# An attention plan with other costs, a model of transfers, 94 shifted due times, and a new front

## The chip, the cores and the metric

One Trainium2 chip, one of its cores. A core has five engines with a queue of instructions each: PE (matmuls), DVE and ACT and POOL (elementwise work), SP (here only the issue of transfers), and 16 DMA engines that move data between HBM and the on-chip memories. PE writes its results to PSUM, the accumulators; POOL reads only the on-chip SBUF. The metric is the device time of one execution in microseconds (us), as a median over runs.

## The reference

One encoder layer on 512 tokens of width 1024, in float32, with 16 learned meta tokens ahead. Two attention mixers run on the same normalised input, their outputs are gated and merged, and a gated feed-forward network follows:

```python
u = rms_norm(h, pre_mix_gain[l])
proj = u @ w_in[l]
qa, ka, va, qb, kb, vb, g = jnp.split(proj, SPLITS, axis=-1)
# rope on qa (16 heads x 64), ka (4 heads), qb and kb (8 heads x 2 x 64)
o_swa = windowed_gqa_sink_attention(qa, ka, va, attn_sink[l], pos, is_real)
o_diff = differential_attention(qb, kb, vb, lam, lambda_init, diff_subln_gain[l], is_key)
gates = jax.nn.sigmoid(g + b_gate[l])
merged = g_swa * (o_swa @ w_branch_swa[l]) + g_diff * (o_diff @ w_branch_diff[l])
h = h + rms_norm(merged @ w_out[l], post_mix_gain[l])
u = rms_norm(h, pre_ffn_gain[l])
gate_up = u @ w_ffn_in[l]
f = (jax.nn.silu(gate_up[..., :D_FF]) * gate_up[..., D_FF:]) @ w_ffn_out[l]
h = h + rms_norm(f, post_ffn_gain[l])
```

The windowed attention has 4 key/value heads for 16 query heads, a band of three 128-blocks, the meta keys and a sink. The differential attention has 8 heads; each takes two softmaxes, subtracts `lam` times the second from the first, multiplies by V and normalises per head.

## The kernel before, in words

**Numbers.** Each float32 operand is split into a high and a low part: a cast on ACT makes the high part (`wh`, `xh`), a subtraction on DVE or POOL the rest (`wl`, `xl`). A product of two split operands is three matmuls (`mm3`, L287 to L289): high by high, high by low, low by high. A projection is eight such steps into one PSUM tile `pr`, of which there are three.

**The front** (up to L505) is written out in order. 60 small matmuls on zeros (L380) run while the first transfers land. x is loaded in eight pieces and split; the K projection of the windowed mixer follows on PE piece by piece, then two V projections (`wV` into two `tr` tiles, `wV2` by `v2`). In parallel the rows of x (`xn`, `xm`) are loaded and squared for the row norm `rst`, which PE transposes into `rps` and ACT copies to `rbc`; V, Q and K need it.

**The plan.** From L505 to the end of the attention nothing is ordered by hand. The code states tasks (`T(engine, cost, function, reads, writes, ...)`) and `Plan.run` plays them through in time: at each step it takes the engine that can start first, and on it the task with the earliest due time among those that can start within 0.12 us. A task's due time is when it can start plus a slack by its priority (on PE the priority alone). The instructions are then emitted in that order, engine by engine, so the costs set the order and nothing else: on the chip each engine goes through its queue and waits where an operand is missing. Each issue of a transfer also waits until the last transfer of one of eight counters, given out in turn over all queues, has landed.

**What the plan orders.** `v_swa` scales, transposes and splits V; `q_swa` and the K block project, rotate (`rope_t`: two multiplications on DVE, an addition on POOL, a high part on ACT, a low part on DVE) and move the result by SP transfers (`move`) into the layout of the scores. In it Q holds its high part in partitions 0 to 63 and its low part in 64 to 127, and K its high and low part side by side, in both halves. `s_swa` and `t_swa` are scores and output of one of 16 block steps of the windowed mixer, `qk`, `vd`, `s_diff`, `t_diff` the same of a head of the differential one. A step of `s_diff` is four matmuls `Sd`, a minimum on DVE (L868), an exponential on ACT (L871), a reciprocal, for the second softmax a multiplication by `nlam` (L881), and the scaling. `t_diff` transposes four blocks `tr` (L918), splits them into `dah` and `dal`, and multiplies them by V (L931, L933). Gate projections, branch products `b1` and the projections of later heads fill PE between them. `weights` loads a 512 KB weight by an SP issue (L527), casts it on ACT (L529) and subtracts on POOL for each second one, on DVE for the others (L253); `wr` has three buffers, so a load waits until the weight three back has been split.

```python
T("SP", 0.35, lambda: sp.dma_start(out=wr.t, in_=src.rearrange("p (k c) -> p k c", k=KT)),
  w=[wr], dep=dep, prio=pr_, land=3.6 if nfill[0] > 3 else 0.3)
T("ACT", 1.05, lambda: act.copy(out=wh.t, in_=wr.t), r=[wr], w=[wh], prio=pr_)
if nfill[0] % 2:
    T("POOL", 2.65, lambda: sub_hi(wl.t, wr.t, wh.t, pool), r=[wr, wh], w=[wl], prio=pr_, port=True)
```

After the plan come the branch product with `w_bd`, the output projection, the norms and the feed-forward network, which the change leaves alone.

Of the kernel before, what the change touches and what calls it, by code (L numbers as in the profile page):

```python
# [109 lines left out]
class Task:  # L110
    def __init__(self, n, eng, cost, fn, prio, port, land):
        self.n, self.eng, self.cost, self.fn, self.prio, self.port, self.land = n, eng, cost, fn, prio, port, land
        self.deps, self.alloc, self.bufs, self.done, self.start = set(), [], [], None, None


class Plan:
# [6 lines left out]
    AFTER = dict(PE=0.22, ACT=0.07, DVE=0.07, POOL=0.12, SP=0.1)  # L123

    def __init__(self, tags, free):
        self.free = free
        self.slots = {t: [0.0] * n for t, n in tags.items()}
        self.tasks, self.sigs, self.bufs, self.last = [], {}, [], {}
# [19 lines left out]
    def task(self, eng, cost, fn, r=(), w=(), dep=(), keep=(), on=(), sig=None, prio=9, port=False, land=0.0,  # L148
             chain=None):
        k = Task(len(self.tasks), eng, cost, fn, prio, port, land)  # L150
# [25 lines left out]
    def run(self):  # L176
        free = self.free
        port = 0.0
        todo = {e: [k for k in self.tasks if k.eng == e] for e in free}
        self.idle = []  # L180
        while any(todo.values()):
            best = None
            for e, ks in todo.items():
                cand = []
                for k in ks:
                    t = 0.0
                    for d in k.deps:
                        if d.done is None:
                            t = None
                            break  # L190
                        t = max(t, d.done + (0.0 if d.eng == e else self.AFTER[d.eng]))
# [5 lines left out]
                    for tag, n in need.items():  # L197
# [4 lines left out]
                        t = max(t, f[n - 1] + 0.07)  # L202
# [4 lines left out]
                    cand.append((max(t, free[e], port if k.port else 0.0), due, k))  # L207
# [30 lines left out]
def encoder(ctx, tc, I, out, dbg=None):  # L238
# [89 lines left out]
    nlam = const.tile([P, 1], F32, name="nlam")  # L328
    qsc = const.tile([P, 1], F32, name="qsc")
# [49 lines left out]
    for _ in range(60):  # L379
# [41 lines left out]
    nw[0] += 1  # L421
# [19 lines left out]
    for k in range(KT):  # L441
        todo = [(ps_, w[a][:, k, :], (xh, xl)[b][:, k, cs], k == 0 and a == b == 0, k == KT - 1 and a == 1)
                for hs, w in ((kA, wA), (kB, wB)) for ps_, cs in zip(hs, halves) for a, b in ((0, 0), (0, 1), (1, 0))]
        if k == 0:
            todo = [x for p in range(3) for x in todo[p::3]]
        for ps_, a, b, first, last in todo:
            pe.matmul(out=ps_, lhsT=a, rhs=b, start=first, stop=last)
# [42 lines left out]
    v2(1, range(KT))  # L490
# [9 lines left out]
    for c in range(2):  # L500
# [9 lines left out]
                   ta=2, tb=1, vt=1, rt=RT, ma=3), dict(PE=4.3, ACT=0.05, DVE=0.05, POOL=0.0, SP=0.0))  # L510
# [10 lines left out]
    def weights(src, dep=()):  # L521
# [5 lines left out]
        T("SP", 0.35, lambda: sp.dma_start(out=wr.t, in_=src.rearrange("p (k c) -> p k c", k=KT)),  # L527
          w=[wr], dep=dep, prio=pr_, land=3.6 if nfill[0] > 3 else 0.3)
        T("ACT", 1.05, lambda: act.copy(out=wh.t, in_=wr.t), r=[wr], w=[wh], prio=pr_)  # L529
        if nfill[0] % 2:  # L530
            T("POOL", 2.65, lambda: sub_hi(wl.t, wr.t, wh.t, pool), r=[wr, wh], w=[wl], prio=pr_, port=True)
        else:
            T("DVE", 1.23, lambda: sub_hi(wl.t, wr.t, wh.t), r=[wr, wh], w=[wl], prio=pr_, port=True)
        return wh, wl

    def products(w, x, xb, c0, c1, dep=()):
# [3 lines left out]
        for k in range(KT):  # L540
            T("PE", 3 * mm_t(c1 - c0),
              lambda k=k: mm3(pb.t[:, 0:c1 - c0], (wh.t[:, k, :], wl.t[:, k, :]),
                              (x[0][:, k, c0:c1], x[1][:, k, c0:c1]), k == 0, k == KT - 1),
              r=[wh, wl] + xb, w=[pb], dep=dep, prio=20 + nfill[0])
        return pb

    def rope_t(hl, pa, pb, c0, n, p0, o0, scale, more=False):

        ta = sb("ta", [P, 2, HALF], F32, "ta", 2)
        tb = sb("tb", [P, 2, HALF], F32, "tb", 1)  # L550
        m = 2 * n / 528.0

        def half(t, src, i):
            dve.tensor_tensor(out=t.t[:, :, 0:n], in0=src.t[:, p0:p0 + n].unsqueeze(1).broadcast_to([P, 2, n]),  # L554
                              in1=rot[:, i:i + 2, c0:c0 + n], op=ALU.mult)
# [8 lines left out]
        T("DVE", 0.15 + 0.55 * m, lambda: half(ta, pa, 1), r=[pa, ROT], w=[ta], prio=3)  # L564
        T("DVE", 0.15 + 0.55 * m, lambda: half(tb, pb, 0), r=[pb, ROT], w=[tb], prio=3)
# [1044 lines left out]
```

## Time and profile before

| | |
|---|---|
| median of 3 runs | 951.69 us (951.49 to 952.1) |
| the profiled execution | 949.22 us |
| its span, first to last instruction | 947.4 us |
| PE busy | 931.6 us, 98% |
| DVE, ACT, POOL busy | 76%, 55%, 23% |
| HBM | 95 GB/s over the span |

Times in the profile count from the span's start. The profiled execution lies 1.8 us above its span and 2.5 us below the median of the runs. A matmul's time runs from its start to the modelled end of its pipeline, and the next one starts before that end, so the sum of their times is more than PE's busy time. PE is 98% busy: what counts is where PE stands idle or starts late, and not how much the other engines do. The granted clock (PEclk) is full in all 40 slices of the page but one stretch, which the windows show.

### The profile page before, as it was taken

Reading aid. Unit: us, or ns where it says so; the run is one execution under the profiler, and the core shown is the slowest. Engines: PE = TensorE matmul, PEld = TensorE weight load, DVE = VectorE, ACT = ScalarE, POOL = GpSimd, SP = SyncE. Lnnn points to the kernel's source line nnn. Section 1 sums busy time; section 2 is a strip of 40 time slices with the busy share of each in tenths; the row PEclk is TensorE's granted clock in tenths of the full one; section 3 lists DMA queues with packets and bytes.
Section 4 is the critical chain, followed back from the end, with each engine's and each line's share of the span. In section 5 each row is a group of like instructions: output and inputs, shape, how many; then the busy total and the mean of one; then the engine's idle time right before and its main releaser. Section 6 shows DMA issues by size and latency. Waiting matters only on the chain.

```text
span 947.4 us, 15653 instructions
## 1 busy us (share of the span) xinstructions
PE 931.6 (98%) x5871; PEld 834.1 (88%) x5871; DVE 716.2 (76%) x1234; ACT 525.8 (55%) x957; POOL 216.0 (23%) x228
## 2 busy tenths in 40 slices
PE   9999999999999999999999999999999999999996
PEld 9788879889898999999888888998999999988885
DVE  5738898999564759877773865886787887799975
ACT  7337766775644446667556443654555555565541
POOL 0544455543222433243211421300000000000000
PEclk9999999999999999999999999999999999999999
DMA  9483132251425144433532460364323333180122
GB/s 319 160 220 102 51 104 58 63 148 45 123 89 157 46 122 127 105 96 115 157 112 67 161 216 23 100 186 141 117 104 101 117 95 112 46 333 13 55 67 89
DMA packets 38011, 110.46 MB, mean 117 GB/s; under 512 B 6177, under 2 KB 7457, under 8 KB 37937
## 3 DMA queue, kind: packets, MB, share of 16 engines
q1 hardware_dynamic: 37792, 109.34, 38.1%
q8 instruction: 46, 0.75, 0.3%
q14 instruction: 29, 0.23, 0.1%
q10 hardware_dynamic: 144, 0.13, 0.0%
HBM read 88.09 MB, written 2.10 MB: 95 GB/s over the span
## 4 chain that ended last, share of the span: by engine, by line
PE 86%; DVE 5%; DMA 4%; ACT 2%; issue 1%; SPq 1%; DVEq 0%; ACTq 0%
PE pr L287 19%; PE pr L289 19%; PE pr L288 19%; PE Sd L863 3%; PE wk L288 2%; PE wk L287 2%; PE wk L289 2%; PE Sw L715 2%; PE O L771 2%; PE tr L918 2%; PE Od L931 2%; PE tr L764 2%; DMA wr<-in_w_in_dram 2%; PE tr L288 1%; PE tr L287 1%; PE tr L289 1%
## 5 line engine op out<-in xcount | busy, mean ns | idle before, releaser
L287 PE MATMUL pr<-xh,wh 128*128 128x264 f32 (+1 forms) x592 | 193.4, 327 | 0.0
L289 PE MATMUL pr<-xh,wl 128*128 128x264 f32 (+1 forms) x592 | 190.0, 321 | 0.6 <-POOL wl L253 0.6
L288 PE MATMUL pr<-xl,wh 128*128 128x264 f32 (+1 forms) x592 | 189.8, 321 | 0.0
L253 POOL TENSOR_TENSOR wl<-wr,wh 128x1024 fp32r<-128x1024 f32 (+2 forms) x42 | 99.5, 2372 | 145.2 <-ACT wh L529 82.5
L289 PEld LDWEIGHTS pr<-xh,wl 128*128 128x128 f32 x592 | 111.6, 189 | 9.6 <-POOL wl L253 1.3
L288 PEld LDWEIGHTS pr<-xl,wh 128*128 128x128 f32 x592 | 111.9, 189 | 7.4
L287 PEld LDWEIGHTS pr<-xh,wh 128*128 128x128 f32 x592 | 111.8, 189 | 7.4 <-issue 0.2
L529 ACT CAST wh<-wr 128x1024 fp32r<-128x1024 f32 x56 | 58.5, 1048 | 47.0 <-PE pr L288 34.6
L309 POOL TENSOR_TENSOR r3y<-r3v,mhalf 128x1 f32<-128x1 f32 x4 | 2.2, 549 | 326.1 <-DVE r3v L308 326.1
L253 DVE TENSOR_TENSOR wl<-wr,wh 128x1024 fp32r<-128x1024 f32 (+2 forms) x61 | 69.0, 1134 | 10.0 <-ACT wh L272 8.2
L287 PE MATMUL pr<-TM,sx 128*128 128x256 f32 x236 | 66.9, 283 | 0.2 <-ACT s L1393 0.2
L289 PE MATMUL pr<-TM,sx 128*128 128x256 f32 x236 | 66.8, 283 | 0.0
L288 PE MATMUL pr<-TM,sx 128*128 128x256 f32 x236 | 66.8, 283 | 0.0
L868 DVE TENSOR_REDUCE nm<-Sd 128x1 f32<-128x528 f32 x64 | 45.1, 705 | 20.8 <-PE Sd L863 19.9
L253 DVE TENSOR_TENSOR sx<-S,sx 128x1024 fp32r<-128x1024 f32 x34 | 41.6, 1224 | 24.9 <-PE pr L288 12.7
L289 PE MATMUL pr<-uh,wl 128*128 128x256 f32 (+1 forms) x188 | 55.0, 292 | 0.4 <-DVE wl L253 0.4
L287 PE MATMUL pr<-uh,wh 128*128 128x256 f32 (+1 forms) x188 | 55.0, 293 | 0.0
L288 PE MATMUL pr<-ul,wh 128*128 128x256 f32 (+1 forms) x188 | 54.9, 292 | 0.0
L566 POOL TENSOR_TENSOR ta<-ta,tb 128x528 f32<-128x528 f32 (+1 forms) x26 | 37.0, 1422 | 74.5 <-DVE tb L554 45.3
L871 ACT ACTIVATE pp<-Sd,nm 128x528 f32<-128x528 f32 x40 | 27.9, 699 | 39.2 <-DVE pa L884 22.6
L257 ACT CAST sx<-S 128x1024 fp32r<-128x1024 f32 x34 | 35.7, 1050 | 25.1 <-PE pr L289 8.2
L729 POOL TENSOR_SCALAR p<-p,rc 128x272 f32<-128x272 f32 (+1 forms) x64 | 35.9, 573 | 47.9 <-DVE rc L727 44.5
(528 smaller groups left out, 2673.9 us busy)
## 6 DMA issues: line engine op xcount, KB each, us to landing
wr<-in_w_in_dram SPq DMA_DIRECT2D x50, 512.0 KB, 4.1
wg<-in_w_fi_dram SPq DMA_DIRECT2D x17, 512.0 KB, 3.6
wu<-in_w_fi_dram SPq DMA_DIRECT2D x17, 512.0 KB, 3.5
wr<-in_w_fi_dram SPq DMA_DIRECT2D x16, 512.0 KB, 3.8
b<-in_w_fo_dram SPq DMA_DIRECT2D x16, 512.0 KB, 8.5
Kd<-hl SPq DMA_DIRECT2D x32, 132.0 KB, 2.4
Kd<-Kd SPq DMA_DIRECT2D x16, 264.0 KB, 3.7
Q<-hl SPq DMA_DIRECT2D x64, 64.0 KB, 2.8
```

What stands on the lines that cost most here:

```text
L253: (eng or dve).tensor_tensor(out=lo, in0=src, in1=hi.bitcast(F32), op=ALU.subtract)
L257: act.copy(out=hi, in_=src)
L287: pe.matmul(out=ps, lhsT=ah, rhs=bh, start=first, stop=False, **more)
L288: pe.matmul(out=ps, lhsT=ah, rhs=bl, start=False, stop=False, **more)
L289: pe.matmul(out=ps, lhsT=al, rhs=bh, start=False, stop=last, **more)
L529: T("ACT", 1.05, lambda: act.copy(out=wh.t, in_=wr.t), r=[wr], w=[wh], prio=pr_)
L566: T("POOL", 0.05 + 1.3 * m, lambda: pool.tensor_tensor(out=ta.t[:, :, 0:n], in0=ta.t[:, :, 0:n], in1=tb.t[:, :, 0:n], op=ALU.add), r=[tb], ...
L715: pe.matmul(out=Sw2[S.slot][:, 0:nk], lhsT=QS[g][hh].t[:, i * P:(i + 1) * P], rhs=KB[g].t[:, x, r0:r1], start=(x == 0), stop=(x == 1))
L729: T("POOL", 0.2 + 0.43 * c, lambda z=z: pool.tensor_scalar(out=pt.t[:, z, 0:nk], in0=pt.t[:, z, 0:nk], scalar1=rc.t[:, z:z + 1], scalar2=1 ...
L863: pe.matmul(out=S.t[:, s, 0:HALF], lhsT=Q[c].t[:, i * P:(i + 1) * P], rhs=K[c].t[:, x, s * HALF:(s + 1) * HALF], start=(x == 0), stop=(x = ...
L868: T("DVE", 0.71, lambda S=S, c=c, one=one: dve.tensor_reduce(out=nm.t[:, c, one], in_=S.t[:, :, 0:HALF], axis=AX.XY, op=ALU.min), r=[S], w ...
L871: T("ACT", 0.9, lambda S=S, c=c, one=one, p=p: act.activation(out=p().rearrange("p (a b) -> p a b", a=2), in_=S.t[:, :, 0:HALF], func=AF.E ...
```

## The change

**Plan.** The cost of nearly every task is another. The single landing time per transfer is replaced by one queue for transfers (`xfer`): each starts 1.2 us after its issue at the earliest, behind the one before, and lands 0.45 us after its service. The delay from engine to engine (`AFTER`) becomes `lag`, with a drain of 0.165 us for PE. 94 tasks get a shift of their due time (`SHIFT`).

**Weights.** From the fourth on, ACT issues the plan's weight loads and no longer SP (55 of 58). POOL's subtraction is cut into four quarters, and a product's k-th step waits for its quarter alone.

**Attention.** K's low part is no longer copied to partitions 64 to 127, and the second score matmul takes partitions 0 to 63 alone, which leaves out the product of the two low parts. The multiplication by `nlam` on DVE becomes a scaling of the denominator by `ilam` = 1/`nlam` on ACT ahead of the reciprocal. The copy of V's meta rows moves from DVE to ACT. K's rotation comes behind V. The first two `w_bd` products stand in the plan, and the second V half's products too.

**Front.** 41 small matmuls for 60; K's weights from an array that the host has laid out anew, both columns of a k together; V's weight in two halves.

```diff
@@ Plan
-    AFTER = dict(PE=0.22, ACT=0.07, DVE=0.07, POOL=0.12, SP=0.1)
+    OVER = dict(PE=0.0, ACT=0.098, DVE=0.083, POOL=0.03, SP=0.0)
+    DRAIN = dict(PE=0.165, ACT=0.0, DVE=0.0, POOL=0.0, SP=0.0)
+    SHIFT = (
+        "39:2.27 71:16 98:-0.25 104:2.63 115:8 178:78 217:6 226:0.81 242:-8 251:2 262:0.35 290:-0.48 292:3.44 "
...
+    def lag(a, b):
+        return (0.77 if a == "SP" else 0.27) if b == "PE" else 0.06 if b == "SP" else 0.092 if b == "POOL" and a in ("ACT", "DVE") else 0.036
...
+                    due += self.shift.get(k.n, 0.0)
...
-            free[k.eng] = t + k.cost
-            k.done = t + k.cost + k.land
+            free[k.eng] = t + max(0.06, k.cost - self.OVER[k.eng]) if k.eng != "PE" else t + k.cost
+            k.done = t + k.cost + k.land + self.DRAIN[k.eng]
+            if k.xfer:
+                queue = max(t + 1.2, queue) + k.xfer
+                k.done = queue + 0.45
@@ front
-    for _ in range(60):
+    for _ in range(41):
         pe.matmul(out=wps[:, 0:P], lhsT=warm, rhs=warm, start=True, stop=True)
...
+    for what in ("x0", "w0", "x1", "x2", "w1", "x3", "x4", "w2", "x5", "x6", "w3", "x7"):
+        n = int(what[1])
+        if what[0] == "w":
+            k_weights(n)
+        else:
+            x_load(n)
+            x_split(n)
...
+    for ks in (slice(0, KT // 2), slice(KT // 2, KT)):
+        sp.dma_start(out=rV[:, ks], in_=I["w_in"][2].rearrange("p (k c) -> p k c", k=KT)[:, ks])
+        split(wV[0][:, ks], wV[1][:, ks], rV[:, ks])
@@ weights
-        T("SP", 0.35, lambda: sp.dma_start(out=wr.t, in_=src.rearrange("p (k c) -> p k c", k=KT)),
-          w=[wr], dep=dep, prio=pr_, land=3.6 if nfill[0] > 3 else 0.3)
+        e, eng, xfer = ("ACT", act, 2.0) if nfill[0] > 3 else ("SP", sp, 0.0)
+        T(e, 0.38, lambda: eng.dma_start(out=wr.t, in_=src.rearrange("p (k c) -> p k c", k=KT)), w=[wr], dep=dep,
+          prio=pr_, land=0.7, xfer=xfer)
...
-            T("POOL", 2.65, lambda: sub_hi(wl.t, wr.t, wh.t, pool), r=[wr, wh], w=[wl], prio=pr_, port=True)
+            parts = []
+            for q in range(4):
+                ks = slice(2 * q, 2 * q + 2)
+                parts.append(T("POOL", 0.69, lambda ks=ks: sub_hi(wl.t[:, ks], wr.t[:, ks], wh.t[:, ks], pool), r=[wr, wh],
+                               keep=[wl], prio=pr_))
@@ K
-        move(lambda K=K: K.t[64:128], lambda K=K: K.t[0:64], [], [K], land=4.0)
+            move(lambda K=K: K.t[64:128, 0], lambda K=K: K.t[0:64, 0], [], [K], 0.7)
@@ s_diff (s_swa likewise)
-                            pe.matmul(out=S.t[:, s, 0:HALF], lhsT=Q[c].t[:, i * P:(i + 1) * P],
-                                      rhs=K[c].t[:, x, s * HALF:(s + 1) * HALF], start=(x == 0), stop=(x == 1))
+                            pe.matmul(out=S.t[:, s, 0:HALF], lhsT=Q[c].t[0:P - 64 * x, i * P:(i + 1) * P],
+                                      rhs=K[c].t[0:P - 64 * x, x, s * HALF:(s + 1) * HALF], start=(x == 0), stop=(x == 1))
...
+                if c:
+                    T("ACT", 0.2, lambda one=one: act.activation(out=den.t[:, 1, one], in_=den.t[:, 1, one], func=AF.Copy,
+                                                                 scale=ilam), w=pw, on=["lam"], prio=0)
...
-                    T("DVE", 0.16, lambda one=one: dve.tensor_tensor(out=rc.t[:, 1, one], in0=rc.t[:, 1, one], in1=nlam,
-                                                                    op=ALU.mult), on=[("r", h, c, i), "lam"],
-                      sig=("m", h, i), prio=0, port=True)
@@ vd
-        T("DVE", 0.22, lambda: dve.tensor_copy(out=m.t[64:80], in_=m.t[0:16]), r=[m], w=[m], prio=2)
+        T("ACT", 0.25, lambda: act.copy(out=m.t[64:80], in_=tm.t[0:NMETA, 0:P]), r=[tm], w=[m], prio=2)
```

**What moves, at three places.** The first is ACT in the front, where x and the first V weight (`wV`) are split and the rows of x (`xn`) are squared. Before, a `wV` cast is followed by the square:

```order
L397 ACTIVATE xh<-xr,vec 128x528 x4
L272 CAST wV<-wr 128x1024
L460 ACTIVATE jk,ss<-xn 128x1024
L467 COPY kraw<-pr 128x264 x3
L467 COPY kraw<-Sw 128x264
```

Now, with what each waits for:

```order
L278 CAST wh<-wr 128x512 [waits DMAHW4_49]
L419 ACTIVATE xh<-xr,vec 128x528 [waits DMAHW5_49]
L278 CAST wV<-wr 128x512 [waits DMAHW6_49]
L558 DMA wr<-in_w_in_dram 128x1024 [waits DMAHW0_49,DVE_49]
L278 CAST wV<-wr 128x512 [waits DMAHW7_49]
L491 ACTIVATE jk,ss<-xn 128x1024 [waits Pool_49]
```

Between the casts of `wV`'s two halves ACT issues a weight load of the plan; it waits for counter 0, whose last transfer is the first piece of `xn`.

The second place is DVE at the plan's start, behind the copies of the row norm: the V tiles (`VT`) are scaled, the rotation table (`rot`) too, and K is rotated (`ta`, `tb`). Before:

```order
L589 TENSOR_TENSOR VT<-tr,rbc 128x264 x2
L653 TENSOR_TENSOR rot<-rot,rbc 128x1584
L554 TENSOR_TENSOR ta<-kraw,rot 128x528
L554 TENSOR_TENSOR tb<-kraw,rot 128x528
L554 TENSOR_TENSOR ta<-kraw,rot 128x528
L589 TENSOR_TENSOR VT<-pr,rbc 128x264 x2
L628 SCALAR_TENSOR_TENSOR Vm<-tr,vec,Vm 128x2x64
```

Now:

```order
L624 TENSOR_TENSOR VT<-tr,rbc 128x264 x2
L691 TENSOR_TENSOR rot<-rot,rbc 128x1584
L274 TENSOR_TENSOR Vs<-tr,Vs 128x8x64
L624 TENSOR_TENSOR VT<-pr,rbc 128x264
L663 SCALAR_TENSOR_TENSOR Vm<-tr,vec,Vm 128x2x64
L624 TENSOR_TENSOR VT<-pr,rbc 128x264
L585 TENSOR_TENSOR ta<-kraw,rot 128x528
L585 TENSOR_TENSOR tb<-kraw,rot 128x528
```

The second V tile's scaling has gone ahead of K's rotation. On PE six products of 512 columns stood between the transposes of the first V tile and those of the second; now 18 of 264 columns, one transpose and six of 512 do.

The third place is PE at the output of the differential mixer's sixth head, from the transposes of its first two blocks. Before:

```order
L918 MATMUL tr<-ident,pa 128x128 x3
L918 MATMUL tr<-ident,pp 128x128
L918 MATMUL tr<-ident,pa 128x128 x3
L918 MATMUL tr<-ident,pp 128x128
L863 MATMUL Sd<-Kd,Qd 128x264 x4
L931 MATMUL Od<-dah,Vd 128x512 x2
L933 MATMUL Od<-dal,Vd 128x512
L931 MATMUL Od<-dah,Vd 128x512 x2
```

Now:

```order
L959 MATMUL tr<-ident,pa 128x128 x3
L959 MATMUL tr<-ident,pp 128x128
L959 MATMUL tr<-ident,pa 128x128 x3
L959 MATMUL tr<-ident,pp 128x128
L308 MATMUL pr<-xh,wh 128x264
L309 MATMUL pr<-xl,wh 128x264
L310 MATMUL pr<-xh,wl 128x264
L308 MATMUL pr<-xh,wh 128x264
L309 MATMUL pr<-xl,wh 128x264
L310 MATMUL pr<-xh,wl 128x264
L903 MATMUL Sd<-Kd,Qd 128x264 x4
L972 MATMUL Od<-dah,Vd 128x512 x2
```

Six projection matmuls have moved in between the transposes and the first product that reads their copy `dah`, and the product of `dal` no longer follows directly. Over the whole attention PE has the same matmuls but for the 19 small ones; 30 more products of 512 columns stand ahead of the first scores of the windowed mixer (183 for 153).

More of the change, by code (lines that the diff above doesn't have):

```diff
@@ L148, in task @@
     def task(self, eng, cost, fn, r=(), w=(), dep=(), keep=(), on=(), sig=None, prio=9, port=False, land=0.0,
-             chain=None):
-        k = Task(len(self.tasks), eng, cost, fn, prio, port, land)
+             chain=None, xfer=0.0):
+        k = Task(len(self.tasks), eng, cost, fn, prio, port or eng == "POOL", land, xfer)
         k.deps.update(dep)
@@ L190, in run @@
                             break
-                        t = max(t, d.done + (0.0 if d.eng == e else self.AFTER[d.eng]))
+                        t = max(t, d.start + d.cost if d.eng == e == "PE" else d.done + self.lag(d.eng, e))
                     if t is None:
@@ L328, in encoder @@
     nlam = const.tile([P, 1], F32, name="nlam")
+    ilam = const.tile([P, 1], F32, name="ilam")
     qsc = const.tile([P, 1], F32, name="qsc")
@@ L441, in encoder @@
     for k in range(KT):
[L442 to L447, printed above, removed]
-    pV = [tr_t()[:, 0:HALF], tr_t()[:, 0:HALF]]
-    for h in range(2):
-        proj(pV[h], wV, X, h * HALF, (h + 1) * HALF)
+        w = [t[:, k % 4] for t in wK[k // 4][1:]]
+        for a, b in ((0, 0), (0, 1), (1, 0)):
+            for n, hs in enumerate((kA, kB)):
+                for ps_, cs in zip(hs, halves):
+                    pe.matmul(out=ps_, lhsT=w[a][:, n, :], rhs=(xh, xl)[b][:, k, cs], start=(k == a == b == 0),
+                              stop=(k == KT - 1 and a == 1))
+    pV = [tr_t()[:, 0:HALF], tr_t()[:, 0:HALF]]
+    for a, b in ((0, 0), (0, 1), (1, 0)):
+        for h in range(2):
+            for k in range(KT):
+                pe.matmul(out=pV[h], lhsT=wV[a][:, k, :], rhs=X[b][:, k, halves[h]], start=(a == b == k == 0),
+                          stop=(a == 1 and k == KT - 1))
     kraw = [atp.tile([P, EXT], F32, tag="q", name="kraw", bufs=8) for _ in range(2)]
@@ L648, in encoder @@
     PV2 = [pl.held("pr", t) for t in pV2]
+    W2 = [pl.held(t, x) for t, x in zip(("wh", "wl"), wV2)]
+    for k in range(KT):
+        T("PE", 0.367, lambda k=k: v2(1, [k]), r=W2, w=PV2[1:], prio=9)
     for b in MK:
@@ L1041, in encoder @@
     gate2((0, 1, 2, 3), "hl", 1, S6[7:8], [heads[7]["moved"]])
+    first = []
+    for j in range(2):
+        wh, wl = weights(I["w_bd"][j], heads[7]["S"][4 + j:5 + j])
+        pb = bank("pr", 3, "pr")
+        for k in range(KT - 1):
+            T("PE", 0.694, lambda k=k, wh=wh, wl=wl, pb=pb: mm3(
+                pb.t, (wh.t[:, k, :], wl.t[:, k, :]), (dd[0][:, k, :], dd[1][:, k, :]), k == 0, False),
+              r=[wh, DD[k]], w=[pb], keep=[wl], dep=[wl.parts[k // 2]], prio=200 + j)
+        for b in (wh, wl, pb):
+            b.left += 1
+        first.append((wh, wl, pb))
     with tc.manual_schedule(engines={mybir.EngineType.DVE, mybir.EngineType.Activation, mybir.EngineType.SP,
@@ L1058, in bd_products @@
             mm3(b[1], (b[0][0][:, k, :], b[0][1][:, k, :]), (dh[:, k, :], dl[:, k, :]), k == 0, k == KT - 1)
-    first = [(load_w(I["w_bd"][j]), pr_t()) for j in range(2)]
-    for b in first:
-        bd_products(b, range(KT - 1))
+    first = [((wh.t, wl.t), pb.t) for wh, wl, pb in first]
     for j in range(KT):
```

187 lines of the change are left out of this document (96 added, 91 removed), and 7 rows, old and new, of the table SHIFT.

## The prediction

> **What bounds the kernel now.** I read the engine totals first, then the stages by windows, cut at the row norm's last transposes, the first scores of the windowed mixer, the first scores of the differential one, and the end of the plan. Then come the waits of PE in each stage. In the second fence a row has: the window, its length, and busy time with instruction count for PE, PE's weight loads, DVE, ACT and POOL; then the granted clock, the DMA share and GB/s.
>
> ```profile
> PE 931.6 (98%) x5871; PEld 834.1 (88%) x5871; DVE 716.2 (76%) x1234; ACT 525.8 (55%) x957; POOL 216.0 (23%) x228
> ```
>
> ```profile
> 0.00:28.33 28.33, 26.76 (x233) 26.35 (x234) 15.65 (x33) 19.42 (x34) 4.03 (x20) 1.00 0.85 300
> 28.33:72.54 44.21, 41.77 (x190) 33.64 (x189) 24.90 (x32) 13.37 (x19) 22.23 (x13) 0.96 0.71 189
> 72.54:205.30 132.76, 131.56 (x744) 111.38 (x745) 118.75 (x329) 96.12 (x243) 67.17 (x104) 1.00 0.33 89
> 205.30:492.40 287.10, 284.91 (x1916) 259.53 (x1915) 209.48 (x397) 163.05 (x319) 87.42 (x67) 1.00 0.38 106
> 492.40:947.40 455.00, 446.63 (x2795) 403.24 (x2793) 347.43 (x445) 233.81 (x344) 35.19 (x26) 1.00 0.35 113
> ```
>
> PE is the bound nearly everywhere, and the change leaves its work as it is but for 19 small matmuls at the start. So it can only win what PE loses: idle time, matmuls that start late behind an operand, and a low clock. Idle are 28.33 − 26.76 = 1.57 us in the front, 44.21 − 41.77 = 2.44 up to the first scores, and 1.20 + 2.19 = 3.39 in the two attention stages. Behind 492.40, half the span, the order is written by hand and does not change. The change acts on the first 492 us alone. DVE is the second engine to look at: in the windowed stage it works 118.75 of 132.76 us, 89%, so anything late there stays late.
>
> Late starts hide in the durations. In the groups below (operation, tiles, shape, count, then busy time and mean ns, then idle time before them) the same shape costs more in the attention than behind it:
>
> ```profile
> L287 PE MATMUL pr<-xh,wh 128*128 128x264 f32 x400 | 115.8, 290 | 0.0
> L288 PE MATMUL pr<-xl,wh 128*128 128x264 f32 x400 | 113.5, 284 | 0.0
> L287 PE MATMUL pr<-xh,wh 128*128 128x512 f32 x192 | 77.6, 404 | 0.0
> L288 PE MATMUL pr<-xl,wh 128*128 128x512 f32 x192 | 76.3, 397 | 0.0
> L287 PE MATMUL pr<-dh,wh 128*128 128x512 f32 x64 | 24.9, 389 | 0.0
> L863 PE MATMUL Sd<-Kd,Qd 128*128 128x264 f32 x256 | 43.4, 291 | 1.1 <-ACT pp L871 0.7 <-issue 0.2
> L931 PE MATMUL Od<-dah,Vd 128*128 128x512 f32 x64 | 20.7, 405 | 0.0
> L933 PE MATMUL Od<-dal,Vd 128*128 128x512 f32 x32 | 13.1, 410 | 0.0
> L771 PE MATMUL O<-ah,Vs 128*128 128x512 f32 x40 | 16.9, 423 | 0.3 <-ACT ma L752 0.2
> L771 PE MATMUL O<-al,Vs 128*128 128x512 f32 x40 | 16.5, 411 | 0.4 <-DVE al L253 0.2
> ```
>
> I take 389 ns (`dh`, which never waits) as the price of 512 columns and 284 as that of 264. The excess is 15 × 192 + 8 × 192 + 6 × 400 + 7 × 256 + 16 × 64 + 21 × 32 + 34 × 40 + 22 × 40 ns = 12.5 us. Of it 1.7 are the half clock shown below, which leaves 10.8. With the idle 3.39, **the pool of the two attention stages is about 14.2 us**.
>
> **The change, part by part.** *The front.* The chain that ends it is not K's.
>
> ```profile
> 0.97 5.48 PE L380 MATMUL wps<-warm 128*128 128x128 bf16 x60 [0.97 <-DVE warm L377]
> 17.16 1.06 ACT L460 ACTIVATE jk<-xn 128x1024 bf16<-128x1024 f32 x1 [0.29 <-DMA xn<-in_x_dram]
> 21.95 1.06 ACT L460 ACTIVATE jk<-xm 16x1024 bf16<-16x1024 f32 x1 [0.75 <-DMA xm<-in_meta_dram]
> 26.40 0.60 PE L484 MATMUL rps<-ident,rb 128*128 128x128 f32 x4
> 0.00:25.00 25.00, 23.43 (x205) 23.02 (x206) 13.79 (x25) 17.46 (x30) 2.96 (x16) 1.00 0.92 324
> ```
>
> The rows of x land up to 21.95, the norm follows, and its transposes come at 26.40. K can start earlier by at most what 19 of the 60 small matmuls take at the row's mean, 19 × 5.48/60 = 1.7 us, and then PE waits for the norm: no gain. A loss can come from the weight load that ACT now issues between the two `wV` casts, as soon as the first piece of `xn` has landed (before 17.16). Its 512 KB at 324 GB/s are 1.6 us of transfers, among rows of x and V weights that the chain waits for, with the DMA engines 92% busy. If all of it lies ahead of `xm`, the front ends 1.6 later; if behind, not at all. I take the middle, **+0.8** (bounds −1.7, if the norm's chain were to follow K's start, and +3.3, the 1.6 with a window at half clock). The Trainium skill, "DMA: Bandwidth & Descriptors", section "Issuing engines are not separate DMA queues", says that transfers run on the same 16 engines and interleave whoever starts them; by it this term would be nearer +1.6 and the sum 944.8. No row here shows two issuing queues busy at once, so neither number is borne out.
>
> *Up to the first scores.* Here one tie of engines costs PE most.
>
> ```profile
> 28.76 3.98 POOL L253 TENSOR_TENSOR wl<-wr,wh 128x1024 fp32r<-128x1024 f32 x1
> 30.53 2.77 DVE L554 TENSOR_TENSOR ta<-kraw,rot 128x528 f32<-128x528 f32 x1
> 34.46 0.76 DVE L589 TENSOR_TENSOR VT<-pr,rbc 128x264 f32<-128x264 f32 x2
> ```
>
> ```profile
> L607 PE MATMUL tr<-ident,VT x8: 270/286/421, 31.4 to 36.1; 128*128 128x128 f32 x8
> ```
>
> ```profile
> 35.62 0.90 PE L607 MATMUL tr<-ident,VT 128*128 128x128 f32 x4 [1.65 <-DVE Vm L628]
> ```
>
> ```profile
> L607 PE MATMUL tr<-ident,VT 128*128 128x128 f32 x40 | 6.5, 283 | 2.1 <-DVE Vm L628 1.7 <-DVE VT L589 0.5
> L715 PE MATMUL Sw<-KK,Q 128*128 128x272 f32 x64 | 13.2, 305 | 0.5 <-DMA Q<-hl 0.5
> L289 PE MATMUL pr<-xh,wl 128*128 128x512 f32 x192 | 76.2, 397 | 0.3 <-POOL wl L253 0.3
> ```
>
> ```profile
> 32.43:35.84 3.41, 1.47 (x7) 0.92 (x7) 3.16 (x7) 0.87 (x4) 2.15 (x3) 1.00 0.47 156
> 35.84:39.25 3.41, 3.41 (x12) 2.72 (x11) 3.32 (x4) 1.25 (x3) 3.41 (x3) 0.50 0.00 0
> ```
>
> POOL's whole weight takes 3.98 us and DVE's first `ta` beside it 2.77; behind it V's second tile is scaled at 34.46, and PE stands 1.65 us. Then it runs one window at half clock, 3.41/2 = 1.7 us lost. With Q's 0.5 and POOL's 0.3 the stage loses 2.44 + 1.7 = 4.15 us. In the new order the second V tile goes ahead of K's rotation. DVE came to `ta` at 30.53; a subtraction, two scalings and the `Vm` step in its place, at about half a microsecond each (two scalings took 0.76), end at about 32.5. PE meets the first transposes 18 matmuls of 264 columns earlier. At 0.23 us a step for 512 columns (two take 0.62 in a row below, one 0.39) 264 columns cost 0.12, so it comes there 2.2 us earlier than the 31.4 of before. From 29.2 the four transposes (0.5), 18 × 0.12 and 6 × 0.23 lead to 33.2, 0.7 us behind the operand. So the wait goes, the empty window with it, and with the 30 more products ahead of the first scores (30 × 0.23 = 6.9 us) Q's wait as well. Something new waits here and there, which I put at 0.65: **−3.5** (bounds −4.15, all of it, and 0, if `ta` beside the quarters holds up others as long).
>
> *The two attention stages.* I take 5.0 of the pool's 14.2, from three places.
>
> First, waits behind one long DVE or POOL step:
>
> ```profile
> 224.26 2.40 POOL L253 TENSOR_TENSOR wl<-wr,wh 128x1024 fp32r<-128x1024 f32 x1 [1.21 <-ACT wh L529]
> 224.60 2.14 DVE L843 CAST Vdm<-Vdm 16x128 fp32r<-16x128 f32 x1
> ```
>
> ```profile
> L881 DVE TENSOR_TENSOR rc<-rc,nlam x32: 148/159/1023, 222.9 to 490.9; 128x1 f32<-128x1 f32 x32
> ```
>
> A copy of 16 rows takes 2.14 us beside POOL's 2.40, and a step of one column, normally 0.159, up to 1.023. Both go to ACT, and POOL works in quarters. The waits that PE shows for it are 0.7 (`Sd`), 0.5 (`VT`) and 0.3 (`wl`): −1.5. Second, the differential output:
>
> ```profile
> 429.82 0.74 PE L863 MATMUL Sd<-Kd,Qd 128*128 128x264 f32 x4
> 430.39 0.64 PE L931 MATMUL Od<-dah,Vd 128*128 128x512 f32 x2
> 431.36 0.62 PE L931 MATMUL Od<-dah,Vd 128*128 128x512 f32 x2
> ```
>
> From 430.39 to 431.36 stand three matmuls of 0.23, so 0.28 us are lost on `dal`. Now six projection matmuls (0.7 us) stand ahead of `dah`. The excess of `Od` is 1.0 + 0.7 = 1.7, and I take all of it. Third, the windowed output, where the order makes the same move: of 1.4 + 0.9 I take four fifths, 1.8. **Together −5.0.** The bounds are −9.5, two thirds of the pool (DVE at 89% keeps the rest), and +3.4, the idle time doubled by the new order.
>
> *What costs nothing.* ACT now issues 55 loads of about the length of the one that it issues at the end:
>
> ```profile
> L1523 ACTq DMA_DIRECT2D out_dram<-f x1: 371/371/371, 943.8 to 943.8; - x1
> ```
>
> That is 55 × 0.37 = 20 us, and ACT is idle 132.76 − 96.12 = 36.6 and 287.10 − 163.05 = 124.1 us in the two stages; what hides it is PE's work, and without cover it would cost as much as the rival below says. The 192 score matmuls on 64 rows have the same columns, and I price a step of 64 rows like one of 128. The halved copy of K, the scaling by `ilam` and the first two `w_bd` products shift work that has cover: the last head's chain now has 69 products of 512 columns beside it, for 60.
>
> The sum is 0.8 − 3.5 − 5.0 = **−7.7 us**. It is made on the profiled execution: 947.4 of span and 1.8 around it are 949.22, so 941.5. The median of the runs lies 2.5 higher, and I carry the difference to it: 951.69 − 7.7 = **944.0**. The measurement can tell about 0.2%, 1.9 us, from no change.
>
> **The rivals.**
>
> *The front loses more.* If ACT's load pushes `xm` back by 1.6 us, PE stands between K and the norm, its activity falls as in the window of 1.47 above, and the next window runs at half clock. That is 0.8 + 1.7 = 2.5 more than the sum: 946.5. For it speaks that K ends earlier; against it that V's products stand there too. The Trainium skill, "TensorE: Matmul & The Clock Gate", Part 1: The HAM clock gate, judges activity in free-running windows of 3.41 us and lets the clock fall after an idle one. The length agrees with the window at 0.50 here, but 1.94 us of idle were enough, so this trace makes the fall likelier than the rule.
>
> *Most late starts go.* T2's 4.15 and 9.0 of the pool: 0.8 − 4.15 − 9.0 = −12.4, 939.3. The new order is wider at nearly every place that I looked at; but DVE at 89% gets no faster, and of its work only short steps go.
>
> *The change does not do what its order says.* The front pays 1.6 + 1.7, the second stage wins its 3.5, and in the attention the late starts only change places: −0.2, 951.5.
>
> *ACT's queue is held by loads: slower.* An issue waits until the buffer `wr` is free, and ACT works in order. SP stood at these issues for POOL's and DVE's subtractions (us in total, times, longest):
>
> ```profile
> SPq L527 <- POOL wl L253: 87.9, 14, 15.5
> SPq L527 <- DVE wl L253: 36.4, 7, 21.1
> ```
>
> 124 us in which nothing else of SP was urgent. On ACT the exponentials of the scores, the splits of `tr` and the casts would queue behind such a wait, and PE behind those. If a tenth of it reaches PE, +12.4 − 7.7 = +4.7: 956.4. It decides from 7.7/124 = 6%. Against it: the plan knows the wait and can place the issue late, as SP's queue let it place it early; for it: with subtractions late on the chip the wait stands where the plan saw none.
>
> **How the numbers follow.** Forecast 0.48, its own range 941.5 to 946.5; front at half clock 0.16; most late starts gone 0.13; no change 0.08; ACT held 0.15. Faster by over 0.2% are the first three: 0.77; within it 0.08; slower 0.15. The range must hold 0.8: it goes from 938.5, below the second rival by the spread of the late starts, to 952.0, which takes in the third, and leaves out ACT held and some of the low end.
>
> **What would show it.** Right: no wait of PE at the second V tile's transposes, and the granted clock full from 28 to 40 us; no DVE copy `Vdm`; `Od` and `O` means near 389; PE idle below 5 us between 28 and 492. Wrong: transposes `rps` after 27.5, a window at 0.50 in the front, long waits of ACT at the loads (L558) ended by `wl`, with PE waiting for ACT's `pp`, `ah` or `wh`; or `dh` itself longer than 389, since then the pool was no late start.

## The result and the profile after

The changed kernel takes 1007.6 us as a median of 4 runs (1007.37 to 1008.27), the kernel before 951.59 beside it. The ratio is 1.059, with a 95% interval of 1.057 to 1.061: the change makes the kernel **5.9% slower**, where 944.0 us was forecast and the range ended at 952.0.

The engine totals of the changed kernel, and its stages by windows, cut at the end of the norm's transposes `rps`, at the first scores of each mixer and at the end of the last differential scores. (In the trace of before, the first and the last cut, 28.33 and 492.40, lie 1.3 and 4.1 us behind these places. PE is busy without a gap from there to the cuts, so its idle time per stage can be compared.)

```profile
PE 995.9 (99%) x5852; PEld 846.7 (84%) x5852; DVE 715.5 (71%) x1194; ACT 538.5 (54%) x997; POOL 243.5 (24%) x316
```

```profile
0.00:27.31 27.31, 25.45 (x203) 24.82 (x204) 15.07 (x32) 16.75 (x30) 3.90 (x19) 1.00 0.86 307
27.31:75.55 48.24, 48.16 (x232) 39.65 (x230) 27.55 (x34) 18.05 (x25) 27.84 (x30) 1.00 0.63 168
75.55:244.52 168.97, 168.64 (x892) 129.54 (x891) 133.72 (x359) 107.39 (x266) 78.32 (x132) 1.00 0.25 71
244.52:547.13 302.61, 302.42 (x1718) 245.43 (x1716) 188.41 (x320) 161.10 (x329) 95.10 (x108) 1.00 0.32 89
547.13:1006.50 459.37, 451.28 (x2815) 407.26 (x2815) 350.71 (x449) 235.28 (x347) 38.32 (x30) 1.00 0.35 114
```

PE has 19 instructions less than before and is busy 64.3 us longer. It stands idle less than before in every stage of the plan (0.08, 0.33 and 0.19 us, for 2.44, 1.20 and 2.19). So no wait took the place of another. The matmuls take longer. The groups of the score matmuls say which (operation, height and width of the stationary operand, shape, count, busy time and mean ns, idle time before them); first the differential scores of before, then those of the change:

```profile
L863 PE MATMUL Sd<-Kd,Qd 128*128 128x264 f32 x256 | 43.4, 291 | 1.1 <-ACT pp L871 0.7 <-issue 0.2
```

```profile
L903 PE MATMUL Sd<-Kd,Qd 64*128 64x264 f32 x128 | 49.3, 385 | 0.0
L903 PE MATMUL Sd<-Kd,Qd 128*128 128x264 f32 x128 | 43.2, 338 | 0.2 <-ACT pp L911 0.2
L903 PEld LDWEIGHTS Sd<-Kd,Qd 128*128 128x128 f32 x128 | 23.9, 187 | 10.2 <-ACT pp L911 0.4 <-ACT pa L911 0.2
L903 PEld LDWEIGHTS Sd<-Kd,Qd 64*128 64x128 f32 x128 | 23.4, 183 | 20.8 <-issue 7.6
```

Both forms have become slower, also those that kept 128 rows (291 to 338 ns). The timeline shows how. First a step of before that stands between products of 512 columns, as PE rows and as rows of the weight loads, then one of the change in the same two views (start, length, operation, count):

```profile
303.60 0.66 PE L863 MATMUL Sd<-Kd,Qd 128*128 128x264 f32 x4
304.09 0.40 PE L287 MATMUL pr<-oh,wh 128*128 128x512 f32 x1
304.32 0.39 PE L288 MATMUL pr<-ol,wh 128*128 128x512 f32 x1
```

```profile
303.38 0.66 PEld L863 LDWEIGHTS Sd<-Kd,Qd 128*128 128x128 f32 x4
303.97 0.19 PEld L287 LDWEIGHTS pr<-oh,wh 128*128 128x128 f32 x1
```

```profile
327.51 1.23 PE L903 MATMUL Sd<-Kd,Qd 128*128 128x264 f32 x4
328.67 0.50 PE L308 MATMUL pr<-oh,wh 128*128 128x512 f32 x1
329.00 0.39 PE L309 MATMUL pr<-ol,wh 128*128 128x512 f32 x1
```

```profile
327.28 0.19 PEld L903 LDWEIGHTS Sd<-Kd,Qd 128*128 128x128 f32 x1
327.72 0.82 PEld L903 LDWEIGHTS Sd<-Kd,Qd 64*128 64x128 f32 x3 [0.25 <-issue]
328.67 0.19 PEld L308 LDWEIGHTS pr<-oh,wh 128*128 128x128 f32 x1
```

Before, the four scores and the product behind them take 304.32 − 303.60 = 0.72 us. The first weight load begins 0.22 ahead of its matmul, while the matmul before still runs. Now they take 329.00 − 327.51 = 1.49. The load of the first 64-row operand begins at 327.72, 0.21 after the first matmul's start, where dense matmuls of 264 columns stand 0.12 apart. The load of the next 128-row product begins at 328.67, with its matmul and not ahead of it. A step goes 128, 64, 128, 64 and then back to 128: four changes of height for 0.77 us, **0.193 us each**. In some 0.09 of it the next matmul starts late, and some 0.10 are the weight load, which lies beside nothing any more (the product after it takes 0.33 to the next start, for 0.23).

There are 4 changes in each of 64 differential steps and 2 in each of 64 windowed ones, 384 in all. Summed over all score steps of the trace, each from its first score to the second matmul behind its last, the spacing is some 75 us above the dense one (75.9 in the expectations below). The kernel got only 56 us slower, so the rest of the change must have won.

### The profile page after: what moved, and what is told of

The parts are those of the page before. It is cut to its first block, busy times and chain, and to the rows that moved or that the text cites. A ratio compares the mean times of both kernels' runs of the same rounds, so it can differ in the third digit from the quotient of the medians.

```text
span 1006.5 us, 15662 instructions
## 1 busy us (share of the span) xinstructions
PE 995.9 (99%) x5852; PEld 846.7 (84%) x5852; DVE 715.5 (71%) x1194; ACT 538.5 (54%) x997; POOL 243.5 (24%) x316
## 4 chain that ended last, share of the span: by engine, by line
PE 94%; DMA 2%; DVE 2%; ACT 1%; issue 1%; SPq 0%; DVEq 0%; ACTq 0%
PE pr L308 21%; PE pr L310 20%; PE pr L309 20%; PE Sd L903 7%; PE Sw L754 4%; PE wk L309 2%; PE O L811 2%; PE wk L308 2%; PE wk L310 2%; PE tr L804 2%; PE tr L959 2%; PE Od L972 2%; PE tr L310 1%; PE tr L308 1%; PE tr L309 1%; DMA wr<-in_w_in_dram 1%
## 5 line engine op out<-in xcount | busy, mean ns | idle before, releaser
L308 PE MATMUL pr<-xh,wh 128*128 128x264 f32 (+1 forms) x592 | 200.4, 339 | 0.7 <-ACT wh L507 0.6
L274 POOL TENSOR_TENSOR wl<-wr,wh 128x256 fp32r<-128x256 f32 (+1 forms) x130 | 122.7, 968 | 145.8 <-ACT wh L560 78.4
L903 PE MATMUL Sd<-Kd,Qd 128*128 128x264 f32 (+1 forms) x256 | 79.1, 361 | 0.2 <-ACT pp L911 0.2
L560 ACT CAST wh<-wr 128x1024 fp32r<-128x1024 f32 x58 | 60.7, 1049 | 33.4 <-PE pr L309 29.5
L274 DVE TENSOR_TENSOR wl<-wr,wh 128x1024 fp32r<-128x1024 f32 (+2 forms) x59 | 68.3, 1160 | 12.8 <-ACT wh L293 7.8
L903 PEld LDWEIGHTS Sd<-Kd,Qd 128*128 128x128 f32 (+1 forms) x256 | 47.3, 185 | 31.0 <-issue 7.6
```

Of the source, the lines that this page charges most:

```text
L274: (eng or dve).tensor_tensor(out=lo, in0=src, in1=hi.bitcast(F32), op=ALU.subtract)
L308: pe.matmul(out=ps, lhsT=ah, rhs=bh, start=first, stop=False, **more)
L903: pe.matmul(out=S.t[:, s, 0:HALF], lhsT=Q[c].t[0:P - 64 * x, i * P:(i + 1) * P], rhs=K[c].t[0:P - 64 * x, x, s * HALF:(s + 1) * HALF], sta ...
```

## The experiments

Three theories stood. **A**: each change of the stationary operand's height between 128 and 64 rows costs about 0.195 us. **B**: a matmul of 64 rows is slow by itself, wherever it stands. **C**, the slower rival of the prediction: ACT's queue is held by weight loads, or the new order costs the time.

**128 rows again (e1_rows128).** All of the change, but the second score matmul has 128 rows in both mixers, and K's low part is copied with the high one:

```diff
-   lhsT=Q[c].t[0:P - 64 * x, i * P:(i + 1) * P], rhs=K[c].t[0:P - 64 * x, x, ...]
+   lhsT=Q[c].t[:, i * P:(i + 1) * P], rhs=K[c].t[:, x, ...]
-   move(lambda K=K: K.t[64:128, 0], lambda K=K: K.t[0:64, 0], [], [K], 0.7)
+   move(lambda K=K: K.t[64:128], lambda K=K: K.t[0:64], [], [K], 0.7)
```

> The whole change, but the second score matmul takes 128 rows again (K's low part is copied to the other rows as before). In the trace of the change the 384 places where the height of the operand goes from 128 rows to 64 or back carry 75.9 us beyond the dense spacing of matmuls. Theory A, the change of height costs about 0.195 us each time: all of it goes, 1007.6 - 75.9 = 932, plus what the slower PE had covered, at most the 15 us that the rest of the change could otherwise not have won: 932 to 946. Theory C, the loss comes from ACT's queue held by the weight loads or from the new order: no large difference, 995 to 1010.

Measured: 942.5 us (941.86 to 943.48, 5 runs) beside 951.82 of before; ratio 0.991 (0.989 to 0.992). Theory C falls: the loads on ACT and the new order are all in this kernel, and it is faster than before. The height accounts for 1007.6 − 942.5 = 65 us, 0.170 for each change. PE has the same order of matmuls in both kernels, so the traces can be laid side by side: the score steps are 68.8 us shorter here. Some 6 of the 75 us stay as late starts at the scores, and about 2 more are lost elsewhere (the spans differ by 66.4). That fits waits which the slow scores had covered: PE is idle 1.82 us in the two attention stages here, for 0.52 in the change. This kernel beats both.

**64 rows in the kernel before (e2_before_rows64).** Only this edit, in `s_swa` and `s_diff` of before:

```diff
-   lhsT=Q[c].t[:, i * P:(i + 1) * P], rhs=K[c].t[:, x, ...]
+   lhsT=Q[c].t[0:P - 64 * x, i * P:(i + 1) * P], rhs=K[c].t[0:P - 64 * x, x, ...]
```

> The kernel before, with only the second score matmul on 64 rows (the product of the two low parts is left out; the copy of K stays). Theory A and theory B (a 64-row matmul itself takes about 0.39 us more): 951.6 + 75.9 = 1027 if PE had no slack, less the up to 15 us of waits that the longer scores cover: 1012 to 1028. Theory C: within 3 us of 951.6.

Measured: 1021.7 us (1020.85 to 1029.14, 4 runs), ratio 1.076 (1.072 to 1.079), 69.9 us more or 0.182 for each change of height. Some 3.4 of it are the clock: behind a wait of 1.89 us three busy windows run at 0.50 in this trace (10.24 us from 474.7), where before has one of 3.41. Without them it is about 0.173. The edit does its harm in either kernel. A and B remain.

**The same matmuls in another order (e3_grouped).** The change with the two loops of a differential step exchanged:

```diff
-   for s in range(2):
-       for x in range(2):
+   for x in range(2):
+       for s in range(2):
            pe.matmul(out=S.t[:, s, 0:HALF], lhsT=Q[c].t[0:P - 64 * x, ...], ...)
```

> The whole change, with the four matmuls of a differential score step in another order: both of 128 rows, then both of 64, so two changes of height instead of four in each of 64 steps. Theory A: 128 changes fewer, 128 x 0.195 = 25 us: 983, up to 988 if waits return. Theory B, a 64-row matmul is slow by itself wherever it stands: 1007, as the change. In the trace A shows 0.12 us from the first to the second matmul of 64 rows, B about 0.3.

Measured: 982.6 us (982.39 to 982.97), 25.0 less than the change, for 128 changes of height less: 0.195 each, as A expected. There are as many 64-row matmuls as in the change, and B, which expected no change, falls. In the trace the first 64-row matmul of a step takes 386 ns and the second 280, like the second of 128 rows (283); these are medians of 64. A step of this kernel:

```profile
320.40 0.84 PE L903 MATMUL Sd<-Kd,Qd 128*128 128x264 f32 x4
321.18 0.50 PE L308 MATMUL pr<-oh,wh 128*128 128x512 f32 x1
321.51 0.40 PE L309 MATMUL pr<-ol,wh 128*128 128x512 f32 x1
```

```profile
320.18 0.85 PEld L903 LDWEIGHTS Sd<-Kd,Qd 128*128 128x128 f32 x4
321.18 0.19 PEld L308 LDWEIGHTS pr<-oh,wh 128*128 128x128 f32 x1
```

From 320.40 to 321.51 are 1.11 us, 0.39 above the 0.72 of before: two changes. The mark that I had named for A, 0.12 us from the first to the second matmul of 64 rows, did not show. The spacing there is about 0.23, since the first one's record begins with its uncovered weight load. The rest of a change stands ahead of it: 0.21 us from the last matmul of the old height to the first of the new, for 0.12. So the sum of the step decides and not this one distance.

**The control for that order (e9_grouped128).** The loops exchanged as above, in the kernel with 128 rows.

> As e1_rows128, with the order of the four matmuls of a differential score step as in e3_grouped: a control for it. Theory A, only changes of height cost: 942.5 within 1 us. If the order itself won the 25 us of e3_grouped against the change: far below 942.

Measured: 943.0 us (942.42 to 943.55). The order of the four matmuls is worth nothing where their heights are equal. Against this kernel, the 256 changes left in e3_grouped cost 39.6 us, only 0.155 each. In the trace of e3_grouped they cost 0.195 each, and part of that is again covered: this kernel has some 6 us of late starts at the same steps.

**K's low rows as zeros (e8_zero_rows).** The product of the low parts can be left out with 128 rows, if the rows are zero. The kernel with 128 rows, with this edit:

```diff
-   move(lambda K=K: K.t[64:128], lambda K=K: K.t[0:64], [], [K], 0.7)
+   move(lambda K=K: (pool.memset(K.t[64:128, 1].bitcast(F32), 0.0), K.t[64:128, 0])[1], lambda K=K: K.t[0:64, 0], [], [K], 0.7)
```

> As e1_rows128, but K's low part is not copied: its rows 64 to 127 are set to zero by POOL ahead of the copy of the high part, so the product of the low parts is left out, as the change has it, and the operand keeps 128 rows. If the halved copy is worth nothing, as predicted, and the zeros are hidden on POOL: 942.5 within 1.5 us, so the change's aim costs nothing without the change of height. If POOL's 12 more steps delay the quarters, as whole subtractions did in e6_pool_whole: 944 to 948, with PE waits for wl from POOL. If the shorter copy helps: 940 to 941.

Measured: 942.6 us (942.36 to 943.35). The halved copy is worth nothing that can be measured, and neither do the zeros cost anything that can (POOL has 20 more steps of about 0.54 us, not the 12 that I expected). So the smaller transfer was never on the path, and only the price of the smaller matmul was real.

**The loads on SP again (e4_sp_issues).** The kernel with 128 rows; `eng` is `sp` for all loads, at the same places.

```diff
-   e, eng, xfer = ("ACT", act, 2.0) if nfill[0] > 3 else ("SP", sp, 0.0)
+   e, eng, xfer = ("ACT", sp, 2.0) if nfill[0] > 3 else ("SP", sp, 0.0)
```

> As e1_rows128 (the change with 128 rows in the second score matmul), but SP issues the weight loads again, at the same places of the order; every other engine's order is the same. If ACT's issues are hidden in its idle time, as predicted, the time is 942.5 within 1.5 us. If ACT is held by them (the rival), it is faster by 2 us or more. If SP's moves of Q and K queue behind the loads, it is slower, and PE shows waits for a transfer at Sw or Sd.

Measured: 942.4 us (941.94 to 943.16). Which of the two queues issues makes no difference here. In the kernel with 128 rows ACT's waits at its loads are mostly short; the row has minimum, median and maximum in ns, first and last start:

```profile
L558 ACTq EVENT_SEMAPHORE  x31: 17/17/1692, 15.8 to 481.8; - x31
```

When SP issues them, it stands much longer (us in total, times, longest):

```profile
SPq L558 <- POOL wl L274: 57.9, 16, 7.3
SPq L558 <- DVE wl L274: 26.4, 10, 8.1
```

I read it so: on ACT each load stands behind work of ACT's own, and the buffer is free when ACT gets there, while SP has little else to do, arrives early and waits. Long waits on an idle queue were no measure of what a busy queue would wait.

**No shifts (e5_no_shift).** The kernel with 128 rows, `due += 0.0` for the 94 shifts.

> As e1_rows128, with the 94 shifts of due times at zero. The stages of e1_rows128 won 4.2 us up to the first scores and 2.3 in the attention. If the shifts carry the gain of the attention: 944 to 947. If the costs and the rest carry it: 942.5 within 1.5 us.

Measured: 961.8 us (960.33 to 963.29), 19.3 more, against at most 4.5 expected: both expectations miss. The two attention stages of this kernel, and two stretches in which the clock fell:

```profile
76.11:215.94 139.83, 133.31 (x768) 111.77 (x766) 123.31 (x335) 97.44 (x250) 69.74 (x119) 1.00 0.29 75
215.94:488.00 272.06, 264.01 (x1779) 241.10 (x1778) 191.75 (x334) 163.63 (x338) 97.51 (x115) 0.98 0.39 108
240.34:243.75 3.41, 3.41 (x11) 2.74 (x11) 2.48 (x6) 2.15 (x7) 0.95 (x2) 0.50 0.69 178
451.97:458.79 6.82, 5.39 (x15) 4.46 (x16) 4.87 (x9) 4.89 (x11) 0.39 (x1) 0.50 0.76 234
```

```profile
PE Sd L903 <- ACT pp L911: 4.1, 3, 2.2
PE tr L642 <- DVE VT L624: 1.9, 1, 1.9
```

The second fence holds two of PE's waits. PE is idle 6.52 and 8.05 us, where the shifted order has 1.77 and 0.05 (rows below), and three windows run at half clock. So idle time is 12.8 us more, and the windows at half clock lose about 4.4 (half of the 8.80 us that PE is busy in them), of 20.7 between the profiled spans. Without the shifts, the new costs and the rest of the change give an order 11 us slower than before's (961.8 for 950.6 beside it); the shifts bring 19 back. Which of them do is open.

**POOL's weight whole (e6_pool_whole).** The kernel with 128 rows; the first quarter's task does all, the others nothing, and PE's order is the same.

```diff
-   parts.append(T("POOL", 0.69, lambda ks=ks: sub_hi(wl.t[:, ks], wr.t[:, ks], wh.t[:, ks], pool), ...))
+   parts.append(T("POOL", 0.69, lambda q=q: sub_hi(wl.t, wr.t, wh.t, pool) if q == 0 else None, ...))
```

> As e1_rows128, with POOL's subtraction of a weight whole, as before, at the place of the first quarter. If the quarters removed the wait up to the first scores: 945 to 947, with PE idle at the second V tile's transposes and a window at half clock. If it was V's place ahead of K's rotation: 942.5 to 944, with DVE's first ta near 2.8 us beside POOL's subtraction and no PE wait for it.

Measured: 952.5 us (951.96 to 953.31, 12 runs), 10 us more, over twice the most that either side expected, and not at the place that they named. The second V tile of this kernel waits for nothing and the clock is full there. Two rows of the timeline, and PE's wait as a whole:

```profile
419.98 2.37 POOL L274 TENSOR_TENSOR wl<-wr,wh 128x1024 fp32r<-128x1024 f32 x1 [2.10 <-ACT wh L560]
```

```profile
422.41 0.39 PE L310 MATMUL pr<-xh,wl 128*128 128x264 f32 x1 [1.28 <-POOL wl L274]
```

```profile
PE pr L310 <- POOL wl L274: 3.1, 4, 1.3
```

The order starts a product when the first quarter of its weight is split. With the whole split, PE's third matmul waits for POOL's end at 422.35, and others of its kind too. These waits are 3.1 us, where PE's idle time grew by 6.6 in all (18.4 for 11.8). A second way is seen on DVE, which takes 727.9 us for 712.3 with the same instructions: the second `ta`, beside POOL's whole subtraction of 2.40, takes 2.65 us for 0.88 (first this kernel, then the one with 128 rows and quarters):

```profile
36.17 2.65 DVE L585 TENSOR_TENSOR ta<-kraw,rot 128x528 f32<-128x528 f32 x1
```

```profile
34.92 0.88 DVE L585 TENSOR_TENSOR ta<-kraw,rot 128x528 f32<-128x528 f32 x1
```

How the 10 us divide between the two is not shown. So the quarters matter all along this order, and not for one wait at its start. Taking them out of this order says what it needs, and not what they would bring to the old one, which wasn't tried.

**60 small matmuls again (e7_warm60).** The kernel with 128 rows and `range(60)`.

> As e1_rows128, with 60 small matmuls at the start for 41. If the norm's chain ends the front, as predicted: 942.5 within 1 us, and the transposes rps at 25.9 as there. If K's start does: rps and the end later by 19 x 0.06 to 19 x 0.11, 1 to 2 us.

Measured: 943.5 us (943.09 to 944.46), 1.0 more, between the two expectations and within what the runs scatter. The transposes `rps` of the norm start at 26.3; in the kernel with 128 rows at 25.9, but with zeros for K's low rows at 26.1, with 128 rows and the grouped order at 26.5 and in the change itself at 26.7, and those four have the same front. So the profiled fronts scatter by 0.8 us, and this run doesn't settle the front.

```profile
L515 PE MATMUL rps<-ident,rb x4: 270/272/273, 26.3 to 26.6; 128*128 128x128 f32 x4
```

## Why the prediction was wrong, by its steps

**The step that failed** stands under what costs nothing: "The 192 score matmuls on 64 rows have the same columns, and I price a step of 64 rows like one of 128." The price was zero; the runs give 65 us in the changed kernel and 70 in the one before. With it fell the premise that the change leaves PE's work as it is but for 19 small matmuls: PE is busy 64.3 us longer. I looked at the columns, which set the time of a dense matmul, and not at its neighbours. The trace of before has no stationary operand of another height than 128 rows, so no row told the price. The Trainium skill has a rule that bears on it: "TensorEngine Tiling (Array Packing)", Tiling Modes, Key Properties, says that a change of the tiling mode drains TensorE. If going from 128 to 64 rows counts as such a change, the trace agrees, with a start 0.09 us late and 0.10 us of uncovered weight load for each; the page states no duration. The missing row should have put the step among the unknown costs with two bounds, and with 384 places even 0.05 us would have outweighed the whole forecast gain. None of the rivals had it either. The one that ended slower put the loss on ACT's queue, and it is not there: with SP's issues the time is the same (942.4 for 942.5). A hold is seen in the front, by the counter that ACT's first load waits for: the cast behind the load comes after 3.33 us of idle time in the changed kernel and 1.82 in the one with 128 rows.

Two readings in the prediction are not as it says. Its first and last cut are not at the norm's transposes and the end of the plan, as said under the result, which changes no idle time. And from the last scores to the first product of `dh`, the traces have 69 products of 512 columns before and 72 after, and to the last `Od` 36 and 27; neither is "69 products of 512 columns beside it, for 60". Nothing in the sum uses that count.

**The other terms** can be read from the kernel with 128 rows, for which 944.0 was in effect the forecast and 942.5 was measured. Its stages, cut as above:

```profile
0.00:26.51 26.51, 24.91 (x203) 24.27 (x204) 14.96 (x32) 16.93 (x30) 3.75 (x19) 1.00 0.87 316
26.51:74.75 48.24, 48.16 (x230) 39.65 (x230) 27.49 (x34) 17.81 (x25) 27.81 (x30) 1.00 0.70 180
74.75:225.02 150.27, 148.50 (x892) 127.86 (x891) 132.01 (x359) 104.59 (x265) 79.43 (x132) 1.00 0.29 81
225.02:480.86 255.84, 255.79 (x1718) 233.14 (x1717) 187.17 (x320) 158.95 (x330) 99.31 (x108) 1.00 0.42 112
```

- *The front, +0.8.* In this kernel `rps` starts at 25.91 for 26.40, −0.5; in the change itself, with the same front, at 26.72, +0.3. So the sign is lost in the scatter of the fronts. The mechanism that the term priced, the extra load ahead of the meta rows, does not show: they are squared at 21.8 in the change, for 21.95 before. In the kernel with 128 rows they are squared 1.13 us earlier than before, and the transposes follow 5.09 later, for 4.45:

```profile
20.82 1.06 ACT L491 ACTIVATE jk<-xm 16x1024 bf16<-16x1024 f32 x1 [0.55 <-DMA xm<-in_meta_dram]
```

- *Up to the first scores, −3.5.* Idle is 0.08 for 2.44 and the clock stays at 1.00, so 2.4 + 1.7 = 4.1 us are gone, nearly the bound. The steps hold in detail: the second V tile was to be ready at 32.5 and PE to arrive at 33.2; the last scaling starts at 31.9 and takes 0.42, and PE starts the second tile's transposes at 32.79, the last of them at 33.1, with no wait. With POOL whole the stage's idle time stays small too (0.40 us), so it is not the quarters that removed this wait. V's place ahead of K's rotation, which the prediction named, fits, but no run tries it alone.

```profile
L642 PE MATMUL tr<-ident,VT x8: 272/272/273, 28.7 to 33.1; 128*128 128x128 f32 x8
L624 DVE TENSOR_TENSOR VT<-pr,rbc x2: 423/423/423, 30.5 to 31.9; 128x264 f32<-128x264 f32 x2
```

```profile
27.47:76.54 49.07, 48.67 (x232) 39.52 (x230) 29.11 (x34) 17.78 (x25) 24.43 (x15) 1.00 0.67 181
```

- *The attention, −5.0.* Idle time went from 3.39 to 1.82 us: −1.6, which is the first part of the term (1.5). The other two parts, 1.7 and 1.8 for late starts at `Od` and `O`, are not there. The groups of the kernel with 128 rows:

```profile
L972 PE MATMUL Od<-dah,Vd 128*128 128x512 f32 x64 | 20.4, 400 | 0.0
L974 PE MATMUL Od<-dal,Vd 128*128 128x512 f32 x32 | 13.8, 431 | 0.0
L811 PE MATMUL O<-al,Vs 128*128 128x512 f32 x40 | 17.3, 432 | 0.0
L811 PE MATMUL O<-ah,Vs 128*128 128x512 f32 x40 | 16.5, 412 | 1.0 <-DVE ot L823 0.6 <-ACT aTm L1057 0.3
```

The high parts are shorter (400 for 405, 412 for 423) and the low ones longer by as much or more (431 for 410, 432 for 411). I read it so: work put in ahead of `dah` moved the lateness on to `dal`, which is made after it. The prediction's own sum over the same groups gives 13.1 us of late starts in this kernel, where before has 10.8. So the pool was no sum that this order won from.

The three readings, −0.5, −4.1 and −1.6, make 6.2 of the 7.3 us between the profiled spans (947.4 and 940.1). The other 1.1 I can't assign. That 942.5 lies so near 944.0 is in part luck: the attention won 3.4 us less than its term, and the front, the second stage and what I can't assign made up for it. The medians of the runs differ by 9.3, and before's own runs scatter by 4 us beside this kernel.

## What to carry to other kernels

Before a matmul's operands are made smaller, count how often the height of the stationary operand changes between neighbours: each change cost 0.155 to 0.195 us here, where a dense matmul of 264 columns takes 0.12. Rows that should not count can be zero at full height, which cost nothing that could be measured here, and where a smaller height is needed, matmuls of one height belong together. A form of instruction that the trace of before doesn't hold has no price there, and zero is a bound for it, not an estimate; times its count it belongs in the range.

## What the runs showed of the hardware

- A change between 128 and 64 stationary rows takes the weight load out of the matmul's shadow, in both directions: 0.193 us a change within a step, 0.195 from 128 changes less in the whole kernel, and 0.155 to 0.182 where part of it is covered or other losses come with it. The moving operand changes from 128 to 64 rows at the same places; the runs don't tell the two apart.
- A narrower operand of full height did no such thing. The eight transposes of V's meta rows have 16 columns instead of 128, between matmuls of 128, and take the same 272 ns as the others above, with 0.109 us to the next start, as between transposes of full width (minimum, median and maximum in ns, of the kernel with 128 rows):

```profile
L637 PE MATMUL tr<-ident,VT x8: 270/272/272, 203.6 to 443.6; 128*16 128x128 f32 x8
```

- The clock fell to 0.50 for three windows of 3.41 us in the kernel without shifts, which has single waits of 1.9 and 2.2 us on PE just ahead. PE was busy 1.56 and 0.98 of the 3.41 us ahead of the two falls, 1.47 ahead of the one in the kernel before, and 1.50 ahead of the one in the kernel before with 64 rows. In the kernel with the shifts it stayed full throughout the plan, where no wait is longer than 0.6.
